# Strassen's sums of weights by their use: T2 ahead of T3, T3 fetched from memory, and the finished token half's norm behind the last operands

## The chip, the cores and the metric

The kernel runs on one core of a Trainium2 chip. The time is the device time of one launch in microseconds; a comparison takes the median of several runs of each kernel on the same chip. The engines are PE (matmuls; its weight loads are listed as PEld), DVE (vector), ACT (scalar), POOL (GpSimd) and SP. DMAs are issued from the queues of SP, ACT and POOL. Each engine works through its own list of instructions in order and waits on semaphores.

## The reference, cut to what matters

A trunk of two layers, 512 tokens of width 1024, in float32. Each layer is a mixer and a SwiGLU FFN, each with a norm before and after and a gate from a conditioning vector. The change touches the last FFN alone, from its second product on:

```python
def swiglu_ffn(h, w_in, w_out):
    gate, up = jnp.split(h @ w_in, 2, axis=-1)
    return (jax.nn.silu(gate) * up) @ w_out
...
        y = swiglu_ffn(h, f_w_in[i], f_w_out[i])
        x = x + gate * rmsnorm(y, norm_g[i, 3])
```

Here `silu(gate) * up` is 512 x 2816 and `w_out` (`w2` in the kernel) is 2816 x 1024.

## The kernel before

All matmuls are float32 products made of three matmuls on operands split in a high and a low part: ACT casts the high part, DVE subtracts it from the value to get the low part, and PE multiplies high by high, low by high and high by low.

The last product is done by a Strassen scheme with seven products in place of eight. The 22 blocks of 128 rows of `w2` make 11 pairs p = 0 to 10. Of a pair, b11 and b12 are the left and right 512 columns of its first 128 rows, b21 and b22 those of the second 128 rows. The tokens are halved likewise, 0 to 255 and 256 to 511; the activations a11 to a22 lie in `raw`, and sums of them are made by DVE in place. The table `PRODUCTS` names the seven products by the PSUM bank they add to and their two operands:

```python
    PRODUCTS = (("A", "b11", "a11"), ("B", "b21", "a12"), ("C", "b22", "a12"), ("A", "b22", "a11"),
                ("D", "b12", "s1"), ("A", "b11", "a21"), ("A", "b21", "a22"))
```

Four of the operands on the weights' side are sums, made in place, on top of blocks that were used already:

- T1: b12 becomes b12 + b11 (`t1`), used by product 4;
- T2: b22 becomes b22 + T1 (`t2_`), used by product 3;
- T3: b11 becomes the original b12 + b22 (`t3`), used by product 5;
- T4: b21 becomes b21 + T2 (`t4`), used by product 6.

Each sum is an accumulating DMA from GpSimd's queue (`add_`, L1657), with nothing computed by an engine. The weights lie in units: units 0 and 1 hold two pairs each, units 2 to 8 one each. Unit 0 to 2 are in tiles `w2t`, 3 and 4 in `w2s`, 5 to 8 in `w2h`, so the tile's name tells the unit in the profile. The sum of a unit of two pairs is one DMA of 512 KB, of one pair 256 KB; a sweep over the nine units is 2.9 MB.

There are 77 steps, each a product for one pair: 6 matmuls of 512 columns, 3 for each of two token tiles. Products with an odd number take pair 4 first (`odd`), the others go from 0 to 10. Two steps make a round n, 39 rounds. Product 3 begins with the second step of round 16, product 5 in round 27, product 6 in round 33. Product 6 adds up in bank A, which product 5 has just left. In a round n PE runs `products([n])` (L1650), then comes `behind(n)`, then `w_prep(n + 4)` splits the weights of round n + 4 (ACT L1615, DVE L1616) and `a_prep(n + 3)` the activations of round n + 3 (ACT L1628, DVE L1629). There are four buffers of split weights, so the weights of round n + 4 are split when PE is done with round n; of split activations three. The last three rounds run together, first token tile 0 of the half, then tile 1.

`behind(n)` holds what is put between the rounds: the issue of the sums, the copies and sums of finished banks (`got`), and, for the first token half, which is done after product 4 in round 27, the norm and the store. `square` gives a tile's sum of squares on ACT (L1722), `mean` and `root` make the factor (L1725, L1728, L1729), `gated` multiplies by the gate (L1732), `x_new` multiplies by the factor, adds to x and stores (L1738, L1739). In round 32 DVE takes product 5 out of bank A (L1779). The order on PE, SP, ACT, DVE and POOL in this phase is the order in which the code is written.

The T3 of before has two parts, both issued in round 2: a plain load of the original b12 over b11, on SP's queue (L1665), and the sum with b22 in the tile. T2 overwrites b22, and so comes behind T3.

Of the kernel before, what the change touches and what calls it, by code (L numbers as in the profile page):

```python
# [17 lines left out]
T = 512  # L18
# [17 lines left out]
def trunk_kernel(  # L36
# [7 lines left out]
    dma = nc.sync.dma_start  # L44
    dma_s = nc.scalar.dma_start
# [1004 lines left out]
    with ExitStack() as ph:  # L1050
# [99 lines left out]
        class Group:  # L1150
# [169 lines left out]
            def root(self):  # L1320
                self.rg = t2("rg")
                act.activation(self.rg, self.ssg, AF.Sqrt, bias=eps_t, scale=1.0 / 256)
# [219 lines left out]
    with ExitStack() as ph:  # L1542
# [14 lines left out]
        def w2_rows(p, n=1):  # L1557
            return w2[2 * p * P:(2 * p + 2 * n) * P, :].rearrange("(i c p) f -> p i c f", p=P, c=2)
# [9 lines left out]
        def b_(i, name, q=None):  # L1568

            t = rows_of[i][int(name[1]) - 1][:, :, slice(0, T) if name[2] == "1" else slice(T, D)]  # L1570
            return t if q is None else t[:, q, :]
# [81 lines left out]
        with tc.manual_schedule(engines={PE_ENGINE, mybir.EngineType.SP, mybir.EngineType.Activation,  # L1653
                                         mybir.EngineType.DVE, mybir.EngineType.Pool}):

            def add_(dst, src):
                pool.dma_start(dst, src, accum_op=ADD)  # L1657

            def t1(i):
                add_(b_(i, "b12"), b_(i, "b11"))  # L1660

            def t3(i):
                u = units[i]
                for q, p in enumerate(u):
                    dma(b_(i, "b11", q), w2_rows(p)[:, 0, 0, T:])  # L1665
                add_(b_(i, "b11"), b_(i, "b22"))

            def t2_(i):
                add_(b_(i, "b22"), b_(i, "b12"))

            def t4(i):
                add_(b_(i, "b21"), b_(i, "b22"))

            load_pair(0)
            for i, f in ((0, 0), (2, 0), (1, 1), (3, 1), (4, 2), (5, 3)):
                rest(i)
                (up if i in (2, 3) else gate)(f, lead_ps[i])
            tiles = []
            K = 2 * NF - 6
            for k in range(K):  # L1680
                if k % 2 == 0 and k < K - 4:
                    load_pair(k // 2 + 1)
                if k in (8, 14, 20):
                    w2_load((8, 14, 20).index(k))
                if k in (K - 4, K - 2):
                    w2_load(3 + (k - K + 4) // 2)
                if k in (K - 12, K - 10, K - 8):
                    t1((k - K + 12) // 2)
                tiles.append(in_chunk(ws[k], h))
                q, j = divmod(k - 3, 4)  # L1690
                if j < 2 and k > 2:
                    gate(4 + 2 * q + j, tiles[k - 1])
                elif k:
                    up(2 + 2 * q + j, tiles[k - 1])
                if k < K - 2:
                    for op in splits[k + 2]:
                        op()
                else:
                    a_prep(k - K + 2)
                    w_prep(k - K + 2)  # L1700
            up(NF - 1, tiles[-1])

            ht = [hp.tile([P, 1, D], F32, tag=f"h{j}", name=f"w2h{j}") for j in range(KD)]
            for i in range(5, len(units)):
                rows_of[i] = (ht[2 * (i - 5)], ht[2 * (i - 5) + 1])
            for c, r in ((0, 0), (0, 1), (1, 0), (1, 1)):
                for i in range(5, len(units)):
                    dma(rows_of[i][r][:, 0, c * T:(c + 1) * T], w2_rows(units[i][0])[:, 0, r, c * T:(c + 1) * T])
            for n in (2, 3):
                w_prep(n)  # L1710
            a_prep(2)
            for i in range(3, len(units)):
                t1(i)

            st = [{"s2": small(2), "s1": small(1), "b1": small(1)} for _ in range(4)]
            spare = {n: rows_of[i][0][:, 0, T:] for n, i in
                     (("junk", 3), ("gg0", 5), ("gg1", 6), ("c22_0", 7), ("c22_1", 8))}
            gg = (spare["gg0"], spare["gg1"])
            got = {}

            def square(t, part, src):
                act.activation(spare["junk"], src, AF.Square, accum_out=st[t]["s2"][:, part:part + 1])  # L1722

            def mean(t):
                dve.tensor_scalar(st[t]["b1"], st[t]["s2"][:, 0:1], 1.0 / D, EPS, MUL, ADD)  # L1725

            def root(t):
                act.activation(st[t]["s1"], st[t]["s2"][:, 1:2], AF.Sqrt, bias=st[t]["b1"], scale=1.0 / D)  # L1728
                dve.reciprocal(st[t]["s1"], st[t]["s1"])  # L1729

            def gated(src, hf, dst):
                dve.tensor_mul(dst, src, gg[hf])  # L1732
                return dst

            def x_new(t, hf, yg, parts=(FULL,), puts=(dma,)):
                for c, put in zip(parts, puts):
                    cx = slice(hf * T + c.start, hf * T + c.stop)
                    dve.scalar_tensor_tensor(xt[t][:, cx], yg[:, c], st[t]["s1"], xt[t][:, cx], MUL, ADD)  # L1738
                    put(out[0, t * P:(t + 1) * P, cx], xt[t][:, cx])  # L1739

            def behind(n):

                if n == 2:
                    for i in range(len(units)):
                        t3(i)
                for i, u in enumerate(units):
                    if n - 8 == u[-1] // 2:
                        t2_(i)
                if n == 18:
                    for i in range(len(units)):  # L1750
                        t4(i)
                for t in range(2):
                    if n == 5:
                        got["11", t] = t2("c11")
                        act.copy(got["11", t], bank["A"][t])
                    elif n == 10:
                        dve.tensor_add(got["11", t], got["11", t], bank["B"][t])
                    elif n == 16:
                        got["12", t] = t2("c12")
                        act.copy(got["12", t], bank["C"][t])  # L1760
                    elif n == 21:
                        dve.tensor_tensor(got["12", t], got["12", t], bank["A"][t], SUB)
                    elif n == 27:
                        dve.tensor_add(got["12", t], got["12", t], bank["D"][t])
                        got["22", t] = spare[f"c22_{t}"]
                        act.copy(got["22", t], bank["D"][t])
                    elif n == 28:
                        square(t, 0, got["11", t])
                        square(t, 1, got["12", t])
                        mean(t)  # L1770
                    elif n == 29:
                        root(t)
                        for hf, c in enumerate(("11", "12")):
                            gated(got[c, t], hf, got[c, t])
                    elif n == 30:
                        for hf, c in enumerate(("11", "12")):
                            x_new(t, hf, got[c, t])
                    elif n == 32:
                        dve.tensor_tensor(got["22", t], got["22", t], bank["A"][t], SUB)  # L1779
                    elif n == 33:  # L1780
                        square(2 + t, 0, got["22", t])
                        mean(2 + t)
                    elif n == 34:
                        gated(got["22", t], 1, got["22", t])

            for n in range(NT - 3):
                products([n])
                behind(n)
                if n == 26:
                    for hf in range(2):  # L1790
                        dma(gg[hf], gate_d[3, 4 * hf:4 * hf + 4].rearrange("j p -> (j p)").partition_broadcast(P))
                if n + 4 < NT:
                    w_prep(n + 4)
                if n + 3 < NT:
                    a_prep(n + 3)
            products(range(NT - 3, NT))
            for t in range(2):
                square(2 + t, 1, bank["A"][t])
                yg = gated(bank["A"][t], 0, t2("yg"))
                root(2 + t)  # L1800
                if t == 0:
                    x_new(2, 0, yg)
                    x_new(2, 1, got["22", 0])
                else:
                    x_new(3, 1, got["22", 1])
                    x_new(3, 0, yg, HALVES, (dma_s, dma))
# [29 lines left out]
```

## Time and profile before

| | us |
|---|---|
| median of 3 runs | 1376.9 (1376.27 to 1377.57) |
| the profiled execution's own time | 1379.01 |
| its span, first to last instruction | 1377.2 |
| PE busy in the span | 1345.5 |
| DVE, ACT, POOL busy | 898.0, 570.4, 46.1 |
| last FFN's second product, first matmul to the last one's end | 1238.8 to 1371.0 |

A row of the timeline gives the start and the length in us, the engine, the line of the code, the operation, the tile written and those read, the shape and the count of instructions; in brackets stands the idle time before it, and what ended it. In the lines of waits stand the sum, the count and the longest. The clock is the share of full speed granted to PE. A plain load of 256 KB by L1708 landed 3.4 to 6.2 us after its issue, one of the 11 loads by L1665 after 5.9 to 10.9 us.

### The profile page before, as it was taken

What the parts mean: (1) busy time and instruction counts of PE and PEld (TensorE: products, weight loads), DVE (VectorE), ACT (ScalarE), POOL (GpSimd) and SP (SyncE); (2) the same over time, 40 slices, a digit from 0 to 9 for tenths busy, and PEclk for the clock granted to TensorE, in tenths of its full rate; (3) what the DMA queues carried; (4) which work ended last, traced back from release to release, by engine and by line L of the source; (5) the groups of instructions that cost most, each with busy time, mean ns of one, the idle gap of its engine ahead of it and who ended that gap; (6) DMA issues with size and microseconds to landing.
All of it is one profiled execution on the core that took longest, in us unless ns stands there. A gap on an engine that the chain in (4) does not pass through costs nothing.

```text
span 1377.2 us, 17423 instructions
## 1 busy us (share of the span) xinstructions
PE 1345.5 (98%) x6909; PEld 1130.4 (82%) x6909; DVE 898.0 (65%) x1437; ACT 570.4 (41%) x893; POOL 46.1 (3%) x59
## 2 busy tenths in 40 slices
PE   8999999999999999999999999999999999999596
PEld 7788889888888888898888888888898888888485
DVE  5578766777876323768988888896743233339366
ACT  5333355232222212745555554564742212126363
POOL 0000000000000000000000000000000000002310
PEclk9999999999999999999999999999999999999798
DMA  9767751777775323333434443223402554249841
GB/s 311 227 189 240 236 178 31 244 227 240 233 248 183 123 92 91 97 100 119 138 108 138 119 126 114 85 91 108 153 31 92 168 168 130 92 131 254 142 85 61
DMA packets 160533, 204.77 MB, mean 149 GB/s; under 512 B 6836, under 2 KB 112196, under 8 KB 159428
## 3 DMA queue, kind: packets, MB, share of 16 engines
q1 hardware_dynamic: 150096, 179.23, 40.8%
q0 software_dynamic: 6208, 11.54, 4.9%
q10 hardware_dynamic: 4148, 12.90, 3.0%
q8 instruction: 54, 0.88, 0.3%
q14 instruction: 27, 0.22, 0.1%
HBM read 189.87 MB, written 2.24 MB: 139 GB/s over the span
## 4 chain that ended last, share of the span: by engine, by line
PE 91%; issue 3%; SPq 2%; DMA 1%; DVE 1%; ACT 1%; POOL 1%; DVEq 0%; POOLq 0%; ACTq 0%
PE ip L276 18%; PE ip L278 18%; PE ip L277 18%; PE y L378 6%; PE y L380 6%; PE y L379 6%; PE li L276 3%; PE li L278 3%; PE li L277 3%; PE cA L1650 2%; PE li L756 1%; PE yd L1283 1%; PE cD L1650 1%; SPq L611 1%; PE yo L1277 1%
## 5 line engine op out<-in xcount | busy, mean ns | idle before, releaser
L276 PE MATMUL ip<-h,whl 128*128 128x512 f32 x1096 | 430.8, 393 | 0.2 <-DVE cv L863 0.2
L278 PE MATMUL ip<-h,whl 128*128 128x512 f32 x1096 | 426.8, 389 | 0.0
L277 PE MATMUL ip<-h,whl 128*128 128x512 f32 x1096 | 426.5, 389 | 0.0
L222 DVE TENSOR_TENSOR whl<-wst,whl 128x1024 fp32r<-128x1024 f32 x132 | 160.7, 1221 | 133.5 <-ACT whl L221 133.4
L276 PEld LDWEIGHTS ip<-h,whl 128*128 128x128 f32 x1096 | 205.8, 188 | 43.7 <-issue 1.8
L278 PEld LDWEIGHTS ip<-h,whl 128*128 128x128 f32 x1096 | 205.7, 188 | 43.5
L277 PEld LDWEIGHTS ip<-h,whl 128*128 128x128 f32 x1096 | 205.9, 188 | 41.8
L221 ACT CAST whl<-wst 128x1024 fp32r<-128x1024 f32 x132 | 136.6, 1042 | 32.1 <-PE ip L278 23.7
L124 DVE SCALAR_TENSOR_TENSOR ada_acc<-ada_st,csil,ada_acc 128x512 f32<-128x512 f32 x140 | 105.0, 750 | 3.8 <-DMA ada_st<-in_ada_w_dram 0.3
L204 DVE TENSOR_TENSOR whlo<-wsto,whlo 128x1024 fp32r<-128x1024 f32 x41 | 49.9, 1224 | 78.4 <-ACT whlo L203 78.2
L276 PE MATMUL li<-h,whl 128*128 128x256 f32 x288 | 83.2, 289 | 0.0
L278 PE MATMUL li<-h,whl 128*128 128x256 f32 x288 | 81.6, 283 | 0.0
L277 PE MATMUL li<-h,whl 128*128 128x256 f32 x288 | 81.5, 283 | 0.0
L203 ACT CAST whlo<-wsto 128x1024 fp32r<-128x1024 f32 x41 | 42.6, 1049 | 76.3 <-PE y L380 74.8
L1650 PE MATMUL cA<-whlo,ao 128*128 128x512 f32 x264 | 64.9, 405 | 5.4 <-DVE w2h L1779 3.4
L378 PE MATMUL y<-whlo,ff 128*128 128x512 f32 x176 | 68.6, 390 | 0.0
L380 PE MATMUL y<-whlo,ff 128*128 128x512 f32 x176 | 68.5, 389 | 0.0
L379 PE MATMUL y<-whlo,ff 128*128 128x512 f32 x176 | 68.5, 389 | 0.0
L1650 PEld LDWEIGHTS cA<-whlo,ao 128*128 128x128 f32 x264 | 51.3, 196 | 18.1 <-issue 4.1
L1142 DVE SCALAR_TENSOR_TENSOR cu<-ip,cols,cu 128x511 f32<-128x511 f32 (+2 forms) x84 | 62.8, 748 | 3.9 <-ACT cu L1139 1.4
L1585 ACT ACTIVATE g<-ip 128x512 f32<-128x512 f32 x18 | 10.8, 598 | 121.9 <-PE ip L278 121.9
L276 PEld LDWEIGHTS li<-h,whl 128*128 128x128 f32 x288 | 55.3, 192 | 0.0
(278 smaller groups left out, 1931.0 us busy)
## 6 DMA issues: line engine op xcount, KB each, us to landing
ada_st<-in_ada_w_dram SPq DMA_DIRECT2D x96, 512.0 KB, 5.3
wst<-in_f_w_in_dram SPq DMA_DIRECT2D x44, 1024.0 KB, 6.4
wst<-in_m_w_in_dram SPq DMA_DIRECT2D x14, 1024.0 KB, 5.3
wsto<-in_f_w_out_dram SPq DMA_DIRECT2D x10, 1024.0 KB, 5.2
wst<-in_m_w_in_dram SPq DMA_DIRECT2D x20, 512.0 KB, 4.9
wst<-in_a_w_in_dram SPq DMA_DIRECT2D x9, 1024.0 KB, 6.1
csb<-cs_d ACTq DMA_DIRECT2D x8, 1024.0 KB, 5.1
wsto<-in_m_w_out_dram SPq DMA_DIRECT2D x7, 1024.0 KB, 6.4
```

Of the source, the lines that this page charges most:

```text
L124: dve.scalar_tensor_tensor(acc, w, csil[:, k:k + 1], acc, MUL, ADD)
L204: dve.tensor_tensor(dst[:, 1, :nk, :], src, dst[:, 0, :nk, :].bitcast(F32), SUB)
L221: later.append((lambda sw=sw, w=w: act.copy(w[:, 0, :nk, :], sw), lambda sw=sw, w=w: dve.tensor_tensor(w[:, 1, :nk, :], sw, w[:, 0, :nk, : ...
L222: lambda sw=sw, w=w: dve.tensor_tensor(w[:, 1, :nk, :], sw, w[:, 0, :nk, :].bitcast(F32), SUB)))
L276: pe.matmul(dst, w_at(w, 0, kk), a[:, 0, sl], start=start, stop=False)
L277: pe.matmul(dst, w_at(w, 0, kk), a[:, 1, sl], start=False, stop=False)
L278: pe.matmul(dst, w_at(w, 1, kk), a[:, 0, sl], start=False, stop=stop)
L378: pe.matmul(pst, a[:, 0, tk], wt[:, 0, kk, :], start=k == 0, stop=False)
L379: pe.matmul(pst, a[:, 0, tk], wt[:, 1, kk, :], start=False, stop=False)
L380: pe.matmul(pst, a[:, 1, tk], wt[:, 0, kk, :], start=False, stop=k == K - 1)
L1142: dve.scalar_tensor_tensor(u[:, sft:], pst[:, :T - sft], w[3 - sft], u[:, sft:], MUL, ADD)
L1650: pe.matmul(bank[r][sub], a[:, al, q, tk], w[:, hl, q, :], start=first and k == 0, stop=last and k == 2, skip_group_check=True)
```

## The change

T2 is issued before T3: `t2_(i)` as before in rounds 8 to 13, but with no T3 ahead of it. T3 no longer reads b22 in the tile: b11 is loaded with the original b12 by ACT's queue (`t3_load`, unit i in round 8 + i), and the sum is with the original b22 fetched from memory, pair by pair, issued in round 17. The norm of tokens 0 to 255 is spread: the squares of tile 0 in round 29, of tile 1 in round 30, `mean`, `root`, `gated` and `x_new` in rounds 34 and 35. And in the rounds from 34 on `behind` comes after `w_prep` and `a_prep`, not ahead of them. The gating of product 6's half, `gated(got["22", t], ...)`, moves from round 34 to round 35.

```diff
             def t1(i):
                 add_(b_(i, "b12"), b_(i, "b11"))
 
+            def t3_load(i):
+                for q, p in enumerate(units[i]):
+                    dma_s(b_(i, "b11", q), w2_rows(p)[:, 0, 0, T:])
+
             def t3(i):
-                u = units[i]
-                for q, p in enumerate(u):
-                    dma(b_(i, "b11", q), w2_rows(p)[:, 0, 0, T:])
-                add_(b_(i, "b11"), b_(i, "b22"))
+                for q, p in enumerate(units[i]):
+                    add_(b_(i, "b11", q), w2_rows(p)[:, 0, 1, T:])
...
             def behind(n):
 
-                if n == 2:
-                    for i in range(len(units)):
-                        t3(i)
                 for i, u in enumerate(units):
                     if n - 8 == u[-1] // 2:
                         t2_(i)
+                    if n == 8 + i:
+                        t3_load(i)
+                    if n == 17:
+                        t3(i)
                 if n == 18:
                     for i in range(len(units)):
                         t4(i)
...
-                    elif n == 28:
-                        square(t, 0, got["11", t])
-                        square(t, 1, got["12", t])
-                        mean(t)
-                    elif n == 29:
-                        root(t)
-                        for hf, c in enumerate(("11", "12")):
-                            gated(got[c, t], hf, got[c, t])
-                    elif n == 30:
-                        for hf, c in enumerate(("11", "12")):
-                            x_new(t, hf, got[c, t])
+                    elif n in (29, 30):
+                        if t == n - 29:
+                            square(t, 0, got["11", t])
+                            square(t, 1, got["12", t])
                     elif n == 32:
                         dve.tensor_tensor(got["22", t], got["22", t], bank["A"][t], SUB)
-                    elif n == 33:
+                    elif n == 34:
                         square(2 + t, 0, got["22", t])
+                        mean(t)
                         mean(2 + t)
-                    elif n == 34:
+                    elif n == 35:
+                        root(t)
                         gated(got["22", t], 1, got["22", t])
+                if n == 35:
+                    for t in range(2):
+                        for hf, c in enumerate(("11", "12")):
+                            x_new(t, hf, gated(got[c, t], hf, got[c, t]))
 
             for n in range(NT - 3):
                 products([n])
-                behind(n)
+                if n < 34:
+                    behind(n)
...
                 if n + 3 < NT:
                     a_prep(n + 3)
+                if n >= 34:
+                    behind(n)
```

GpSimd's queue behind the last T1, before. The tiles of units 0 to 2 read the same for T3 and T2, so the first three rows are T3 of units 0 to 2; of the `w2h` tiles the even ones hold b11 and b12, the odd ones b21 and b22, so a row into `w2h0` from `w2h1` is T3, and one into `w2h1` from `w2h0` is T2:

```order
L1657 DMA w2h6_9875<-w2h6_9875 128x512
L1657 DMA w2t0_8556<-w2t0_8556 128x2x512
L1657 DMA w2t1_8557<-w2t1_8557 128x2x512
L1657 DMA w2t2_8558<-w2t2_8558 128x512
L1657 DMA w2s_9736<-w2s_9736 128x512
L1657 DMA w2s_9797<-w2s_9797 128x512
L1657 DMA w2h0_9869<-w2h1_9870 128x512
```

And now, behind the same last T1, from the fourth unit on:

```order
L1657 DMA w2s_9797<-w2s_9797 128x512
L1657 DMA w2h1_9870<-w2h0_9869 128x512
L1657 DMA w2h3_9872<-w2h2_9871 128x512
L1657 DMA w2h5_9874<-w2h4_9873 128x512
L1657 DMA w2h7_9876<-w2h6_9875 128x512
L1657 DMA w2t0_8556<-in_f_w_out_dram 128x512 x2
L1657 DMA w2t1_8557<-in_f_w_out_dram 128x512 x2
L1657 DMA w2t2_8558<-in_f_w_out_dram 128x512
```

The nine sums of T2 stand where T3's nine stood, and T3's eleven follow with memory as their source; T4 follows them as it followed T2.

ACT's list in rounds 7 to 10, the difference (L1615 splits weights, L1628 activations):

```order
 L1615 CAST whlo<-w2t_8556 128x1024
 L1628 CAST ao<-raw 128x512
+L1664 DMA w2t_8556<-in_f_w_out_dram 128x512 x2
 L1615 CAST whlo<-w2t_8557 128x1024
 L1628 CAST ao<-raw 128x512
+L1664 DMA w2t_8557<-in_f_w_out_dram 128x512 x2
 L1615 CAST whlo<-w2t_8558 128x512
 L1615 CAST whlo<-w2s 128x512
 L1628 CAST ao<-raw 128x512
+L1664 DMA w2t_8558<-in_f_w_out_dram 128x512
```

The loads of T3, eleven in all, now stand between ACT's casts, one unit a round.

DVE's list at its end, before, from the last split of weights (`x_102` and `x_103` are the token tiles 2 and 3, `cA` bank A):

```order
L1616 TENSOR_TENSOR whlo<-w2h_9876,whlo 128x512
L1629 TENSOR_TENSOR ao<-raw,ao 128x512
L1629 TENSOR_TENSOR ao<-raw,ao 128x256
L1732 TENSOR_TENSOR yg<-cA_9925,w2h_9869 128x512
L1729 RECIPROCAL ss<-ss 128x1
L1738 SCALAR_TENSOR_TENSOR x_102<-yg,ss,x_102 128x512
```

And now, from the last split of activations on (`x_100` and `x_101` are the token tiles 0 and 1):

```order
L1629 TENSOR_TENSOR ao<-raw,ao 128x256
L1731 RECIPROCAL ss<-ss 128x1
L1734 TENSOR_TENSOR w2h_9873<-w2h_9873,w2h_9871 128x512
L1731 RECIPROCAL ss<-ss 128x1
L1734 TENSOR_TENSOR w2h_9875<-w2h_9875,w2h_9871 128x512
L1734 TENSOR_TENSOR c_10045<-c_10045,w2h_9869 128x512
L1740 SCALAR_TENSOR_TENSOR x_100<-c_10045,ss,x_100 128x512
L1734 TENSOR_TENSOR c_10290<-c_10290,w2h_9871 128x512
L1740 SCALAR_TENSOR_TENSOR x_100<-c_10290,ss,x_100 128x512
L1734 TENSOR_TENSOR c_10047<-c_10047,w2h_9869 128x512
L1740 SCALAR_TENSOR_TENSOR x_101<-c_10047,ss,x_101 128x512
```

Two reciprocals, six gatings and four `x_new` stand ahead of the first gating of the last two token tiles, where nothing stood before.

## The prediction

> **What bounds the kernel now.** I read the page first, then who waited for whom on PE and ACT, then the timelines of PE, POOL, ACT and DVE over the last FFN's second product, then the granted clock by windows. From the page:
>
> ```profile
> span 1377.2 us, 17423 instructions
> PE 1345.5 (98%) x6909; PEld 1130.4 (82%) x6909; DVE 898.0 (65%) x1437; ACT 570.4 (41%) x893; POOL 46.1 (3%) x59
> PEclk9999999999999999999999999999999999999798
> ```
>
> PE works in 98% of the span; only in slices 38 and 39 of 40 does its clock fall, so whatever this change can give lies there. PE's waits from 1238 us on are three, and ACT's longest stands behind the first:
>
> ```profile
> PE cC L1650 <- ACT ao L1628: 14.8, 1, 14.8
> PE cA L1650 <- DVE w2h L1779: 3.4, 1, 3.4
> PE cA L1650 <- DVE ao L1629: 2.0, 1, 2.0
> ACT whlo L1615 <- DMA w2t<-w2t: 18.4, 1, 18.4
> ```
>
> On PE's timeline the first row is the restart after the long wait; 63 matmuls then take 14.28 us (1316.42 to 1330.70), 0.2267 us each; the last row ends at 1371.0:
>
> ```profile
> 1294.59 6.33 PE L1650 MATMUL cC<-whlo,ao 128*128 128x512 f32 x15 [14.82 <-ACT ao L1628]
> ...
> 1316.42 14.44 PE L1650 MATMUL cD<-whlo,ao 128*128 128x512 f32 x63
> 1330.70 0.84 PE L1650 MATMUL cA<-whlo,ao 128*128 128x512 f32 x3
> ...
> 1353.52 17.48 PE L1650 MATMUL cA<-whlo,ao 128*128 128x512 f32 x66 [3.41 <-DVE w2h L1779]
> ```
>
> PE stopped at 1294.59 - 14.82 = 1279.77, with rounds 0 to 14 done. Steps 30 to 76 remain: 47 x 6 = 282 matmuls, 63.9 us, so an unhindered PE would end at 1343.7. It ends 27.3 us later: 20.25 us of waits, and about 7 us of slow clock, which the windows show (busy us of PE, PEld, DVE, ACT, POOL; then clock, DMA share, GB/s):
>
> ```profile
> 10.00:13.40 3.40, 2.01 (x27) 1.60 (x28) 2.13 (x7) 1.95 (x7) 0.00 (x0) 1.00 1.15 307
> ...
> 1283.50:1300.00 16.50, 5.41 (x13) 4.13 (x14) 4.93 (x7) 4.16 (x7) 7.39 (x8) 0.50 0.86 145
> ...
> 1346.60:1348.00 1.40, 1.36 (x6) 1.12 (x7) 1.40 (x3) 0.27 (x1) 0.00 (x0) 1.00 0.00 0
> 1348.10:1358.20 10.10, 6.69 (x16) 4.76 (x16) 7.80 (x14) 3.10 (x7) 0.00 (x0) 0.50 0.28 104
> ```
>
> After each wait PE runs at half clock for 5 to 7 busy us. One such stretch costs some 2.8 us: the 15 matmuls from 1294.59 to the next row at 1300.76 need 3.4 us at full clock.
>
> **T2 ahead of T3 on GpSimd's queue.** The sums today (first row T3 of unit 0, next T3 of 1 and 2; 1281.61 is T2 of unit 0, next T2 of 1 and 2; the last is T4 of unit 0):
>
> ```profile
> 1258.22 1.22 POOL L1657 DMA_DIRECT2D w2t<-w2t  x1 [3.27 <-DVE whlo L1616]
> 1266.38 2.16 POOL L1657 DMA_DIRECT2D w2t<-w2t  x2 [6.94 <-DVE whlo L1616]
> ...
> 1281.61 1.22 POOL L1657 DMA_DIRECT2D w2t<-w2t  x1 [2.27 <-issue]
> 1286.99 2.17 POOL L1657 DMA_DIRECT2D w2t<-w2t  x2 [4.16 <-issue]
> ...
> 1302.05 1.22 POOL L1657 DMA_DIRECT2D w2t<-w2t  x1 [2.28 <-issue]
> ```
>
> A sweep of 2.9 MB takes 20.4 us (1281.61 to 1302.05), 1.86 us for each 256 KB. T2 stands a whole sweep behind T3, and ACT at round 12 waits for T2 of unit 2:
>
> ```profile
> 1274.37 0.62 ACT L1615 CAST whlo<-w2h 128x512 fp32r<-128x512 f32 x1 [1.06 <-PE cC L1650]
> 1293.40 0.62 ACT L1615 CAST whlo<-w2t 128x512 fp32r<-128x512 f32 x1 [18.41 <-DMA w2t<-w2t]
> ...
> 1261.88 1.22 DVE L1616 TENSOR_TENSOR whlo<-w2t,whlo 128x1024 fp32r<-128x1024 f32 x1
> ...
> 1255.50:1261.50 6.00, 6.00 (x29) 4.95 (x28) 5.89 (x11) 3.89 (x7) 1.22 (x1) 1.00 1.08 325
> ```
>
> In the new order T2 of unit 0 waits only for the last reader of b22 there, DVE's split for product C, which ends at 1261.88 + 1.22 = 1263.1. From T2 of unit 0 to ACT's release there are 11.8 us now (1281.61 to 1293.40). Alone, it would land at 1275.0. The upper end: beside SP's loads (the window above moves 325 GB/s, the DMA engines full) T3 of unit 0 held up the next for 8.2 us (1258.22 to 1266.38) against 5.4 for T2's (1281.61 to 1286.99); 11.8 x 8.2 / 5.4 = 17.9, landing at 1281.0. PE comes to round 15 at 1279.77 and started 1.2 us after the cast (1293.40 to 1294.59), so the cast must start by 1278.6. The lateness is -3.6 to +2.4 us. ACT now issues the T3 loads, 512 KB in rounds 8 and 9 and then 256 KB a round of 2.72 us, 94 GB/s, under a third of that window's rate: nearer to the lower end. I enter 0.5 us. Later units have more room: T2 of unit 8 follows a sweep later, by about 1283 (1263.1 + 20.4), and lands near 1288, when round 17 asks for it, two rounds before PE does.
>
> **T3 and T4 behind it.** T3 then runs from about 1285 to 1305, T4 to 1326 with its last landing at 1331. Round r ends at 1274.3 + 2.72 (r - 12). T3's last unit is cast in round 28 (1317.8), T4's in round 34 (1334.1), and PE needs each about 4 us later: 12 and 7 us to spare, if a sum with its source in memory goes at the pace of one within the chip. No row shows such a sum. The bounds are 1.86 us, the pace above, and the landing time, if they go one by one:
>
> ```profile
> w2h<-w2h POOLq DMA_DIRECT2D x16, 256.0 KB, 5.0
> ```
>
> I take 1.86: the sums move the same pieces, and plain loads from memory ran faster than the sums (325 GB/s). Up to 2.5 us the slack covers it.
>
> **Loads on ACT's queue.** 11 issues at about 0.35 us (the ACTq row below). ACT idles 1.06 us in a round (bracket of the 1274.37 row), two issues take 0.7: hidden, and if not, ACT is late by tenths against two rounds of split weights. Taking them from SP gains nothing: no one waits for SP there. POOL gets two more sums to issue and is 3% busy.
>
> **The norm of tokens 0 to 255.** Squares, root and gating leave rounds 28 to 30:
>
> ```profile
> 1340.60 1.28 ACT L1728 ACT_TABLE_LOAD   x1
> 1341.90 0.48 ACT L1728 ACTIVATE ss<-ss 128x1 f32<-128x1 f32 x2
> ...
> 1342.31 1.27 DVE L1732 TENSOR_TENSOR c<-c,w2h 128x512 f32<-128x512 f32 x2
> ...
> 1346.50 2.73 DVE L1738 SCALAR_TENSOR_TENSOR x<-c,ss,x 128x512 f32<-128x512 f32 x4
> ...
> 1316.38 1.27 DVE L1762 TENSOR_TENSOR c<-c,cA 128x512 f32<-128x512 f32 x2
> ```
>
> That takes the 2.0 us wait, and most of the 3.4. What is late next is round 33, where product T4 reuses bank A while DVE must first read it (L1779). In round 21, with no norm about, the same read began at 1316.38, when PE was free at 1316.42: its first half ends 0.64 later, so a PE that needed the bank would wait 0.8 us with a semaphore's 0.15. The far end is today's 3.4. The squares stay in rounds 29 and 30, two in each, 1.5 us by their rows (1336.05 and 1336.80 start the first two) against 1.06 of idle:
>
> ```profile
> 1336.05 0.63 ACT L1722 ACTIVATE w2s<-c 128x512 f32<-128x512 f32 x1
> ...
> 1336.80 0.63 ACT L1722 ACTIVATE w2s<-c 128x512 f32<-128x512 f32 x1
> ```
>
> So DVE, which follows ACT, is up to 0.8 us later by round 31: I take 1.6 us, nearer to round 21's row.
>
> **The tail.** What left the rounds now stands on DVE ahead of the last two tiles:
>
> ```profile
> 1364.23 0.41 ACT L1628 CAST ao<-raw 128x256 fp32r<-128x256 f32 x1 [1.58 <-PE cA L1650]
> ...
> 1368.42 0.69 DVE L1732 TENSOR_TENSOR yg<-cA,w2h 128x512 f32<-128x512 f32 x1 [3.31 <-ACT w2s L1722]
> ...
> 1369.88 0.74 DVE L1738 SCALAR_TENSOR_TENSOR x<-w2h,ss,x 128x512 f32<-128x512 f32 x1
> 1371.76 0.69 DVE L1732 TENSOR_TENSOR yg<-cA,w2h 128x512 f32<-128x512 f32 x1 [1.13 <-ACT w2s L1722]
> ...
> 1373.22 0.87 DVE L1738 SCALAR_TENSOR_TENSOR x<-yg,ss,x 128x256 f32<-128x256 f32 x2
> ...
> 1373.73 0.35 ACTq L1739 DMA_DIRECT2D out_dram<-x  x1
> ```
>
> The last cast starts 6.8 us before PE's end (1364.23, 1371.0). From it: 0.4 + 1.3 table + 0.3 root = 2.0; two reciprocals and two gatings 1.5; four gatings and four x_new 2 x 1.27 + 2.73 = 5.3; tile 2 2.2 (1368.42 to 1370.6); tile 3 2.3 (1371.76 to 1374.1). That is 13.3, some 0.2 less for overlapping ends: DVE ends 6.3 us after PE, where it was 3.1. Bounds: 5.5 and 7. Behind DVE the last store takes the same 3.1 us (1374.1 to 1377.2).
>
> **The sum.** 1343.7 + 0.5 + 1.6 + 6.3 + 3.1 = 1355.2, 22.0 us under this span. The profiled execution took 1379.0 us in all, 2.1 over the runs' median of 1376.9; its own time would be 1357.0, the median 1354.9.
>
> **Rivals.** (1) T2 is late by the full 2.4 us: the price is 2.4 - 0.5 + 2.8 for the clock, 1359.6. For it: T3's 8.2 us beside loads; against: a third of the load. (2) The 1.6 us at round 33 halve the clock: +2.8, 1357.7. For it: after the 2.0 us wait at 1344.6 the clock was still 1.00 in 1346.60:1348.00 and 0.50 from 1348.1; against: in 10.00:13.40 PE worked 2.01 of 3.40 us and kept 1.00. The Trainium skill, "TensorE: Matmul & The Clock Gate", section "HAM oscillation — how this bites in real kernels", warns of PE gaps over about 3.4 us only. By that rule this rival falls and the time stays 1354.9; the trace disagrees, a 2.0 us wait was enough, so the rival keeps its chance. (3) Sums from memory take 3.7 us: T3 ends at 1326, T4's last lands at 1351, 13 us after PE needs it; with one slow stretch +16, 1371. (4) The other side: they go one by one, 5.0 us each. T3 ends at 1340, T4's last lands at 1365.5, 27.5 us late; with two slow stretches +33, 1388, slower. It decides from about 4 us a sum on (11 x (4.0 - 1.86) - 7 = 17 us late, and 5.6 for the clock). Against both: no row hints that memory is the slower source. (5) T2 starts no earlier than now, because POOL is held by something other than T3: the long wait stays and only the norm's waits go (2.0 + 1.8 + 3.4 of clock, less 3.2 of tail), 1372.9. Against: the order leaves only DVE and sums eight places earlier before it.
>
> **Chances.** Forecast 0.58; (1) 0.17; (2) 0.12; (3) 0.06; (4) 0.04; (5) 0.03. The range runs from 1352 (no wait at rounds 15 and 33, tail 5.5) to 1361.5 (rivals 1 and 2 in part together), leaving 3, 4, 5 and some edges out. A difference of 0.2%, 2.8 us, is what a measurement can tell from none: faster 0.94, same 0.02, slower 0.04.
>
> **What would show it.** Right: no PE wait of over 3 us after 1238; T2 of unit 0 at about 1263 on POOL, T3 from about 1285; clock 1.00 to the end; PE ending near 1346, DVE 6 us behind. Wrong: ACT waiting for a sum anywhere; POOL's T3 rows more than 2.5 us apart; a clock of 0.50 before the end; DVE's list ending later than 7 us after PE.

## The result, and the profile after

The changed kernel takes 1357.14 us (median of four runs, 1356.92 to 1357.37) where the kernel before, beside it, took 1377.24 (1376.27 to 1377.61): a ratio of 0.9855, with a 95% interval of 0.9838 to 0.9872. It is faster by 20.1 us. The profiled execution took 1357.08 us, with a span of 1355.3.

The page of the changed kernel, its span, its engines and the granted clock in 40 slices:

```profile
span 1355.3 us, 17419 instructions
PE 1339.1 (99%) x6909; PEld 1126.9 (83%) x6909; DVE 898.7 (66%) x1437; ACT 570.1 (42%) x893; POOL 47.0 (3%) x61
PEclk9999999999999999999999999999999999999998
```

The clock no longer falls in slice 38, and PE is busy 6.4 us less for the same 6909 matmuls: what went there is work at half clock. PE's waits from 1235 us on, and ACT's for sums of weights (in all, count, longest):

```profile
PE cA L1650 <- ACT whlo L1615: 0.8, 1, 0.8
PE cC L1650 <- ACT ao L1628: 0.3, 1, 0.3
```

```profile
ACT whlo L1615 <- DMA w2t<-w2t: 3.9, 1, 3.9
ACT whlo L1615 <- DMA w2h<-w2h: 2.7, 4, 1.7
```

Of 20.2 us of waits on PE 1.1 are left. ACT still waits 3.9 us for a sum; PE feels 0.3 of it. PE's timeline around the two places:

```profile
1279.95 4.05 PE L1650 MATMUL cC<-whlo,ao 128*128 128x512 f32 x15 [0.33 <-ACT ao L1628]
1283.84 0.84 PE L1650 MATMUL cA<-whlo,ao 128*128 128x512 f32 x3
...
1330.33 15.22 PE L1650 MATMUL cA<-whlo,ao 128*128 128x512 f32 x66 [0.77 <-ACT whlo L1615]
```

PE stopped at 1279.62. The next 15 matmuls need 3.40 us at 0.2267 each, and the row behind them starts at 1283.84, 4.22 later: round 15 lost 0.8 us in all, with the clock full, since its operands came piece by piece: PE's weight loads wait 0.75 us for ACT's cast of the activations and then 0.51 us more for DVE's low part. PE ends at 1345.55. GpSimd's queue, the first three T2 rows, the ends of T3 from memory and of T4:

```profile
1263.40 1.22 POOL L1657 DMA_DIRECT2D w2t<-w2t  x1 [10.84 <-DVE whlo L1616]
1272.34 2.16 POOL L1657 DMA_DIRECT2D w2t<-w2t  x2 [7.71 <-DVE ao L1629]
...
1288.88 0.89 POOL L1657 DMA_DIRECT2D w2t<-in_f_w_out_dram  x1 [1.58 <-issue]
...
1308.66 0.86 POOL L1657 DMA_DIRECT2D w2h<-in_f_w_out_dram  x1 [3.33 <-issue]
1312.10 1.22 POOL L1657 DMA_DIRECT2D w2t<-w2t  x1 [2.58 <-issue]
...
1329.36 0.86 POOL L1657 DMA_DIRECT2D w2h<-w2h  x1 [0.46 <-issue]
```

T2 of unit 0 starts when DVE's split is done, and holds up the next for 8.9 us (1263.40 to 1272.34). The eleven sums from memory take ten steps in 19.78 us, 1.98 us each. And ACT's cast of T2 of unit 2, which waited for it, and of the last T4, which did not; then DVE's end, the reading of bank A first:

```profile
1278.76 0.62 ACT L1615 CAST whlo<-w2t 128x512 fp32r<-128x512 f32 x1 [3.91 <-DMA w2t<-w2t]
...
1336.07 0.62 ACT L1615 CAST whlo<-w2h 128x512 fp32r<-128x512 f32 x1 [1.06 <-PE cA L1650]
```

```profile
1329.50 1.28 DVE L1775 TENSOR_TENSOR w2h<-w2h,cA 128x512 f32<-128x512 f32 x2
...
1347.72 0.68 DVE L1734 TENSOR_TENSOR yg<-cA,w2h 128x512 f32<-128x512 f32 x1
1351.30 0.88 DVE L1740 SCALAR_TENSOR_TENSOR x<-yg,ss,x 128x256 f32<-128x256 f32 x2
```

DVE ends at 1352.18, 6.6 us behind PE, and the last store 3.1 us later.

### The profile page after: what moved, and what is told of

It reads as the page before. It is cut to its first block, busy times and chain, and to the rows that moved or that the text cites. A ratio compares the mean times of both kernels' runs of the same rounds, so it can differ in the third digit from the quotient of the medians.

```text
span 1355.3 us, 17419 instructions
## 1 busy us (share of the span) xinstructions
PE 1339.1 (99%) x6909; PEld 1126.9 (83%) x6909; DVE 898.7 (66%) x1437; ACT 570.1 (42%) x893; POOL 47.0 (3%) x61
## 4 chain that ended last, share of the span: by engine, by line
PE 93%; issue 2%; SPq 2%; DMA 1%; DVE 1%; ACT 1%; POOL 0%; DVEq 0%; POOLq 0%; ACTq 0%
PE ip L276 19%; PE ip L278 18%; PE ip L277 18%; PE y L378 6%; PE y L379 6%; PE y L380 6%; PE cA L1650 3%; PE li L276 3%; PE li L278 3%; PE li L277 3%; PE li L756 1%; PE yd L1283 1%; PE cD L1650 1%; SPq L611 1%; PE yo L1277 1%
## 5 line engine op out<-in xcount | busy, mean ns | idle before, releaser
L1650 PE MATMUL cA<-whlo,ao 128*128 128x512 f32 x264 | 61.1, 390 | 0.8 <-ACT whlo L1615 0.8
```

The lines of the kernel that those rows point to most:

```text
L1650: pe.matmul(bank[r][sub], a[:, al, q, tk], w[:, hl, q, :], start=first and k == 0, stop=last and k == 2, skip_group_check=True)
```

## The experiments

A ratio is against the kernel before, run beside each on the same chip (medians there 1377.77 for the first four, 1377.25 for the others).

**The sums alone.** The changed kernel with the norm where it stood before (the cut shows its first part; `x_new`, the last half's norm and the place of `behind` are put back likewise):

```diff
-                    elif n in (29, 30):
-                        if t == n - 29:
-                            square(t, 0, got["11", t])
-                            square(t, 1, got["12", t])
+                    elif n == 28:
+                        square(t, 0, got["11", t])
+                        square(t, 1, got["12", t])
+                        mean(t)
+                    elif n == 29:
+                        root(t)
+                        for hf, c in enumerate(("11", "12")):
+                            gated(got[c, t], hf, got[c, t])
...
```

> The changed kernel with the old norm: tokens 0 to 255 are squared in round 28, rooted in 29, stored in 30, and behind(n) comes ahead of the splits again. Theory (the sums' order took the long wait and its slow clock; the norm was a separate, small matter): no PE wait at round 15 beyond 0.5 us, but the old waits at rounds 31 to 33 come back, 2.0 and 3.4 us, with a stretch at half clock that costs about 3.4, while the tail shrinks from 6.6 to 3.1 us behind PE's end. PE ends at 1345.6 + 5.4 + 3.4 - 0.8 = 1353.6, the span is 1359.8, the time 1361.6. Rival (the norm's waits were a late echo of the long wait, since everything behind it ran late, and go with it): no wait over 1 us at rounds 31 to 33, PE ends at 1345, the span is 1351, the time 1353, better than the change.

It took 1361.6 us (1361.01 to 1362.01), ratio 0.9882 (0.9868 to 0.9897), with a span of 1359.2. PE's waits:

```profile
PE cA L1650 <- DVE w2h L1782: 2.8, 1, 2.8
PE cA L1650 <- DVE ao L1629: 2.0, 1, 2.0
```

The long wait is gone, and the two that stand behind the norm are there, as in the kernel before: the theory holds, and the norm's waits were no echo of the long one. Most of the gain, some 16 us, is the sums'. Against the changed kernel's span 3.9 us more: waits 4.8 for 1.1, two windows at half clock with 6.6 us of PE's work in them (half of which, 3.3, is lost), less 3.5 of the tail (DVE ends 3.1 us behind PE here, 6.6 there), which makes 3.7 + 3.3 - 3.5 = 3.5; 0.4 us of the difference stay without an account.

**The norm alone.** The kernel before with the norm spread as in the changed one:

```diff
-                    elif n == 28:
+                    elif n in (29, 30):
+                        if t == n - 29:
...
-                    elif n == 34:
+                    elif n == 35:
+                        root(t)
                         gated(got["22", t], 1, got["22", t])
+                if n == 35:
+                    for t in range(2):
+                        for hf, c in enumerate(("11", "12")):
+                            x_new(t, hf, gated(got[c, t], hf, got[c, t]))
```

> The kernel before with the new place of the norm alone; T3 stands ahead of T2 as it did. Theory: the 14.8 us wait at round 15 stays with its slow clock (2.8 us), the waits of 2.0 and 3.4 us become one of 0.8, their slow clock goes, the tail grows by 3.5 us: the span falls from 1377.2 by 5.4 - 0.8 + 3.4 - 3.5 = 4.5 to 1372.7, the time is about 1373 to 1374. Rival (what the tail takes is all that the rounds gain): within 1 us of the kernel before.

It took 1372.52 us (1372.25 to 1373.61), ratio 0.9961 (0.9947 to 0.9975). PE's waits:

```profile
PE cC L1650 <- ACT ao L1628: 14.6, 1, 14.6
PE cA L1650 <- ACT whlo L1615: 0.8, 1, 0.8
```

The span is 1371.8, where 1372.7 were expected, and the rival, no gain, falls. So the norm's move takes the 2.0 us away and 0.8 remains of the other, with or without the sums' new order. The parts give 16.2 and 5.3 us by their medians, some 21.4 together, and the whole 20.1: they add up within the intervals, which are about 2 us to either side for each.

**T3 from memory, but ahead of T2.** The changed kernel with T3's loads on SP and its sums issued in round 2:

```diff
-                    dma_s(b_(i, "b11", q), w2_rows(p)[:, 0, 0, T:])
+                    dma(b_(i, "b11", q), w2_rows(p)[:, 0, 0, T:])
...
+                if n == 2:
+                    for i in range(len(units)):
+                        t3_load(i)
+                        t3(i)
                 for i, u in enumerate(units):
                     if n - 8 == u[-1] // 2:
                         t2_(i)
-                    if n == 8 + i:
-                        t3_load(i)
-                    if n == 17:
-                        t3(i)
```

> The changed kernel with T3 fetched from memory as now, but with its loads on SP's queue and its sums on GpSimd's issued in round 2, ahead of T2, as before. Theory (it is the order on GpSimd's queue): T2 of unit 0 is issued at 1279 to 1283 in place of 1263.4, PE waits 13 to 16 us at round 15 and loses 2.8 to the clock, the span is 1355.3 + 13 to 18 = 1368 to 1373, the time 1370 to 1375. Rival (it is the source: T2 had waited for T3 to read b22 in the tile, and a T3 from memory leaves T2 free wherever it stands): T2 goes beside it, no wait over 3 us, the time stays near 1357 to 1360.

It took 1371.6 us (1371.42 to 1373.14), ratio 0.9958 (0.9943 to 0.9973). PE's wait, and on POOL the first T3 and the first T2:

```profile
PE cC L1650 <- ACT ao L1628: 12.9, 1, 12.9
```

```profile
1255.90 0.88 POOL L1657 DMA_DIRECT2D w2t<-in_f_w_out_dram  x1 [1.48 <-DVE ao L1629]
...
1279.23 1.22 POOL L1657 DMA_DIRECT2D w2t<-w2t  x1 [2.80 <-issue]
```

T2 comes as late as forecast, the wait is a little under the 13 to 16 us expected, and the rival, the source, falls. What the sums gain is the order on the queue. The source in memory gives little by itself: 1371.6 us beside 1372.52 for the norm alone, and a wait of 12.9 for 14.6. Its part is to let T2 overwrite b22 before T3.

**T3's loads earlier.** Two mechanisms could have held up T2 of units 1 and 2 by 8.9 us: the loads on ACT's queue beside it, or DVE, named as POOL's releaser. In the changed kernel only the rounds of the loads are moved:

```diff
-                    if n == 8 + i:
+                    if n == (3, 4, 5, 5, 6, 6, 7, 7, 7)[i]:
                         t3_load(i)
```

> The changed kernel with the eleven loads of T3 issued by ACT in rounds 3 to 7, while GpSimd's queue is nearly empty, in place of rounds 8 to 16. Theory (T2 of unit 0 held up the next for 8.9 us, 1263.40 to 1272.34, since the loads share the DMA engines with it): that interval falls to 5.4 to 6 us, T2 of unit 2 lands by 1275.5, the 0.33 us wait at round 15 and the half microsecond of late low parts behind it go; the span falls by 0.8 us to 1354.5, the time to 1356.3. All later sums come 3 us earlier and ACT's waits for sums go. Rival (DVE, busy without a break until 1269, holds back GpSimd's descriptors): the interval stays 8 to 9 us, the wait stays, the time stays at 1357.1.

It took 1355.9 us (1355.6 to 1356.22), ratio 0.9841 (0.9827 to 0.9856). T2 on POOL, ACT's wait, and PE's only wait:

```profile
1263.48 1.22 POOL L1657 DMA_DIRECT2D w2t<-w2t  x1 [10.27 <-DVE whlo L1616]
1269.37 2.16 POOL L1657 DMA_DIRECT2D w2t<-w2t  x2 [4.67 <-DVE c L1760]
```

```profile
ACT whlo L1615 <- DMA w2t<-w2t: 0.9, 1, 0.9
```

```profile
PE cA L1650 <- ACT whlo L1615: 0.8, 1, 0.8
```

The second T2 now starts 5.9 us after the first, not 8.9, with DVE busy for 5.2 of these 5.9 us: the loads slowed the sum, DVE did not hold the queue. ACT waits 0.9 us for a sum, PE waits for none, and PE ends 0.85 us earlier (1344.70). The gain is read from the two profiles; the intervals of the two ratios overlap.

**The tail taken apart.** On top of that kernel, the gating and the roots of tokens 0 to 255 go to rounds 33 and 34, and only `x_new` and the gating of product 6's half stay in round 35:

```diff
-                        mean(t)
...
+                if n in (33, 34):
+                    t = n - 33
+                    if n == 33:
+                        mean(0)
+                        mean(1)
+                    for hf, c in enumerate(("11", "12")):
+                        gated(got[c, t], hf, got[c, t])
+                    if n == 33:
+                        root(0)
+                        root(1)
                 if n == 35:
                     for t in range(2):
                         for hf, c in enumerate(("11", "12")):
-                            x_new(t, hf, gated(got[c, t], hf, got[c, t]))
+                            x_new(t, hf, got[c, t])
+                    for t in range(2):
+                        gated(got["22", t], 1, got["22", t])
...
-                if n < 34:
+                if n < 33:
...
-                if n >= 34:
+                if n >= 33:
```

> The kernel with the early loads, and the first half's norm spread over the rounds: mean, root and the gating of tile 0 in round 33, the gating of tile 1 in round 34, the four x_new and the gating of product 6's half in round 35, all behind the rounds' splits. Theory (the tail, 6.6 us behind PE's end where it was 3.1, is DVE's twelve operations behind the last operands): DVE has 4.2 us of it left in the 6.8 us until PE's end, the tail goes back to 3.1 us, PE's end stays at about 1344.7; the span falls by 3.5 us from 1354.4 to 1350.9, the time from 1355.9 to 1352.4. Rival (four gatings of 0.6 us in rounds 33 and 34 are more than DVE has to spare there, about 0.8 us a round, and PE waits for split operands): a wait of 1 us or more in rounds 35 to 38, a gain under 2 us.

It took 1353.08 us (1352.7 to 1353.53), ratio 0.9825 (0.9812 to 0.9838): 2.8 us under the kernel it starts from, where 3.5 were expected. The two were measured on different chips, on which the kernel before differs by 0.5 us; the spans of the two profiles differ by 3.3 (1354.4 and 1351.1). PE ends at 1344.33, and its only wait is 0.8 us as before, so the rival falls. DVE's timeline at the end:

```profile
1339.64 2.74 DVE L1740 SCALAR_TENSOR_TENSOR x<-c,ss,x 128x512 f32<-128x512 f32 x4
1342.29 1.29 DVE L1734 TENSOR_TENSOR w2h<-w2h,w2h 128x512 f32<-128x512 f32 x2
...
1345.62 0.68 DVE L1734 TENSOR_TENSOR yg<-cA,w2h 128x512 f32<-128x512 f32 x1
...
1347.07 0.88 DVE L1740 SCALAR_TENSOR_TENSOR x<-yg,ss,x 128x256 f32<-128x256 f32 x2
```

The tail falls from 6.6 to 3.6 us (1347.95 less 1344.33). It does not reach 3.1, because DVE still works without a break up to the last tile's gating; the next of its work would have to leave round 35 too.

**Bank A read earlier.** The trace names a cast of ACT (L1615) as what ended the 0.77 us in round 33, the prediction named DVE's reading of bank A. On top of the last kernel, `a_prep(34)` goes ahead of the weights' splits in round 32, out of round 31's list:

```diff
+                if n == 32:
+                    a_prep(34)
                 if n + 4 < NT:
                     w_prep(n + 4)
-                if n + 3 < NT:
+                if n + 3 < NT and n != 31:
                     a_prep(n + 3)
```

> The same, and in round 31 the split of activations for round 34 is put off behind DVE's reading of bank A in round 32. Theory (PE's 0.8 us wait at round 33 is DVE's backlog of one split, 0.6 us, ahead of that reading, although the trace names an ACT cast): the wait falls from 0.78 to about 0.2 us, the span by 0.6 us against the kernel with the norm spread. Rival (it is the cast that the trace names, L1615, split weights that come late): the wait stays at 0.7 to 0.8 us and the time is the same.

It took 1352.54 us (1352.03 to 1353.81), ratio 0.9822 (0.9808 to 0.9835), the lowest of all, though the runs overlap with those of the kernel it starts from. PE's only wait, then its last restart, the reading of bank A and ACT's cast:

```profile
PE cA L1650 <- DVE w2h L1775: 0.2, 1, 0.2
```

```profile
1328.92 15.22 PE L1650 MATMUL cA<-whlo,ao 128*128 128x512 f32 x66 [0.17 <-DVE w2h L1775]
...
1328.09 1.38 DVE L1775 TENSOR_TENSOR w2h<-w2h,cA 128x512 f32<-128x512 f32 x2
...
1328.79 0.62 ACT L1615 CAST whlo<-w2s 128x512 fp32r<-128x512 f32 x1 [1.05 <-PE cA L1650]
```

The wait falls when DVE's list in front of the reading is shorter, and now the trace names DVE. PE stops at 1328.75 here, 0.66 us after the reading began; in the kernel with the norm spread it stopped at 1328.32, 0.05 after (1328.27). ACT's cast did not move: it starts 0.04 us after PE's stop in both (1328.79 and 1328.36), and here PE goes on before the cast ends. The wait fell by 0.6 us as forecast, but the span fell by 0.2 and not by 0.6: in this profile PE was 0.43 us later already at the start of product C (1268.75 against 1268.32), ahead of what was changed. In the changed kernel too the times fit the reading: it starts at 1329.50, its first half ends 0.64 later, and PE goes on at 1330.33.

**The kernel before, twice more.** The saving against the median came out 1.9 us under the forecast though the sum for the span was right, so the question was whether the price of a wait is a constant. Nothing is edited.

> The kernel before, unchanged, for another profile. The execution that the prediction's sum was made against took 1379.0 us, 1.3 us more than any of the runs listed beside it. Theory A (the clock's raising after a wait falls on a grid of about 3.4 us, so the same waits cost more in one execution than in another; the prediction took one execution's price): the waits are 14 to 15, 2.0 and 2.8 to 3.4 us as before, but the stretches at half clock differ by 1 us or more, and so does the span, between 1374.5 and 1377.5. Theory B (T2's landing varies): the wait at round 15 differs by 1 us or more. Theory C (all executions under the profile carry the 2 us, and the changed kernel's too): span 1377.2 and time 1379.0 again.

> The same once more, a third execution of the kernel before, with the same three theories: A, other lengths of half clock with the same waits; B, another wait at round 15; C, again 1377.2 and 1379.0.

They took 1379.31 and 1376.4 us. PE's restarts after the three waits, in the first and then in the second:

```profile
1294.59 6.52 PE L1650 MATMUL cC<-whlo,ao 128*128 128x512 f32 x15 [14.45 <-ACT ao L1628]
...
1346.83 2.55 PE L1650 MATMUL cA<-whlo,ao 128*128 128x512 f32 x10 [2.01 <-DVE ao L1629]
...
1353.71 17.58 PE L1650 MATMUL cA<-whlo,ao 128*128 128x512 f32 x66 [4.34 <-DVE w2h L1779]
```

```profile
1293.95 5.10 PE L1650 MATMUL cC<-whlo,ao 128*128 128x512 f32 x15 [14.30 <-ACT ao L1628]
...
1344.75 4.13 PE L1650 MATMUL cA<-whlo,ao 128*128 128x512 f32 x10 [2.01 <-DVE ao L1629]
...
1351.63 16.80 PE L1650 MATMUL cA<-whlo,ao 128*128 128x512 f32 x66 [2.75 <-DVE w2h L1779]
```

The same 2.01 us wait, and the ten matmuls behind it take 2.55 us in the one and 4.13 in the other. The granted clock says why. In windows of 3.413 us, laid on the instants at which it changes (busy us of PE, PEld, DVE, ACT, POOL, then clock, DMA share, GB/s), the first window of each holds all or most of the 2.0 us wait; first the profile of before that the prediction used, then the first new one, then the second:

```profile
1344.66:1348.07 3.41, 1.44 (x6) 1.20 (x7) 3.41 (x6) 2.21 (x5) 0.00 (x0) 1.00 0.00 0
1348.07:1351.49 3.42, 2.04 (x6) 1.03 (x4) 3.42 (x6) 1.35 (x3) 0.00 (x0) 0.50 0.81 307
1351.49:1354.90 3.41, 1.38 (x3) 1.17 (x4) 3.41 (x7) 1.76 (x5) 0.00 (x0) 0.50 0.00 0
```

```profile
1345.08:1348.49 3.41, 1.66 (x7) 1.41 (x8) 3.41 (x5) 1.98 (x4) 0.00 (x0) 1.00 0.05 20
1348.49:1351.90 3.41, 0.89 (x4) 0.39 (x3) 3.41 (x6) 1.66 (x3) 0.00 (x0) 1.00 0.77 287
```

```profile
1341.31:1344.72 3.41, 1.43 (x6) 0.68 (x5) 3.41 (x7) 3.41 (x7) 0.00 (x0) 1.00 0.00 0
1344.72:1348.14 3.42, 3.39 (x8) 2.72 (x9) 3.42 (x5) 0.25 (x1) 0.00 (x0) 0.50 0.57 213
1348.14:1351.55 3.41, 0.73 (x3) 0.26 (x2) 3.41 (x7) 1.69 (x4) 0.00 (x0) 1.00 0.25 94
```

Where PE was busy for 1.43 or 1.44 us of a window, the next ran at half clock; where it was busy for 1.66, the next stayed full. In the second new profile PE works a whole window at half clock, and the one after it is full again; in the profile of before the half-clock window itself held only 2.04 us of work, and the next stayed at half. So the clock's changes do fall on a grid, as theory A has it, and a 2.0 us wait does not always halve the clock. What A said of the waits missed: the last is 4.34 us in the first new profile, where 2.8 to 3.4 were expected. B falls, since the waits at round 15 (14.82, 14.45, 14.30) differ by half a microsecond, and C falls with the 1376.4 us.

The half clock on those ten matmuls cost nothing, though. From the restart after the 2.0 us wait to the last restart there are 6.89, 6.88 and 6.88 us in the three profiles (1346.63 to 1353.52, 1346.83 to 1353.71, 1344.75 to 1351.63): whatever PE loses there it waits less for DVE, whose reading of bank A begins 6.05 to 6.06 us after the first of the two restarts in all three. The executions part elsewhere, behind the long wait. These are the windows in which PE restarts there, in the same order, all of them at half clock:

```profile
1293.46:1296.87 3.41, 2.28 (x5) 1.70 (x6) 2.64 (x4) 3.41 (x6) 2.40 (x3) 0.50 0.97 163
```

```profile
1293.88:1297.29 3.41, 2.70 (x6) 2.04 (x7) 3.07 (x5) 3.41 (x7) 1.98 (x3) 0.50 1.07 180
```

```profile
1293.52:1296.94 3.42, 2.99 (x7) 2.29 (x8) 3.25 (x6) 3.40 (x6) 1.75 (x3) 0.50 1.07 180
```

Behind the first two, with 2.28 and 2.70 us of work, the next window stayed at half clock; behind the third, with 2.99, it was full. So the 15 matmuls take 6.17, 6.36 and 4.94 us up to the next row (1300.76, 1300.95 and 1298.89), and in the same way the last 66 take 17.48, 17.58 and 16.80.

The times follow these two stretches. PE ends at 1371.0 in the profile that the prediction used, at 1371.29 and 1368.43 in the two new ones: 27.3, 27.6 and 24.7 us behind an unhindered PE. Of these, waits are 20.2, 20.8 and 19.1 (14.3, 2.0 and 2.8 in the last), and the rest, 7.1, 6.8 and 5.6, is mostly clock. The executions took 1379.0, 1379.3 and 1376.4 us, 8.0 us behind PE's end each time. Of the 2.9 us between the two new ones the two stretches make 2.2 (1.42 and 0.78), an earlier stop before the long wait 0.5.

That the other executions of the kernel before differ for the same reason is not shown; only their mean granted clock is on record. It fits: of the 17 beside the experiments, the seven at 0.992, as in the 1376.4 us profile, took 1376.34 to 1377.91 us, six of them 1377.04 or less, and the ten at 0.989 or 0.991 took 1377.25 to 1378.84. But it is not the only thing that moves the time: the last kernel above, at 0.999 in all four runs, spreads from 1352.03 to 1353.81.

## Why the prediction was right, and where it was off

- The order on the queue: right. T2 of unit 0 starts at 1263.4 (1263.1 forecast), and its third unit is cast at 1278.76, within 1275.0 to 1281.0. That cast was 0.2 us behind the 1278.6 worked out; round 15 lost 0.8 us where 0.5 was entered. Rival 1's mechanism, the loads beside the sums, is real: T2's step is 8.9 us with the loads and 5.9 without, from T2 of unit 0 to the cast there were 15.4 us, between the bounds of 11.8 and 17.9, and not nearer the lower one, as the prediction had put it. It had judged by 256 KB of loads a round, but rounds 8 and 9 carry 512 KB each, and just these stand beside T2 of unit 0: all DMAs together moved 196 GB/s from 1263.40 to 1266.10, and 92 in the 5.9 us of the kernel with the loads early. The price of the lateness at round 15 was a third of the rival's 2.4 us.
- T3 from memory: right. 1.98 us a sum, beside the 1.86 taken and far from the 3.7 and 5.0 of rivals 3 and 4. T3 began at 1288.9, not at 1285, since T2 was slowed; T4's last row, at 1329.4, was still early enough, for ACT's cast of round 34 waited for PE alone. Issuing the loads on ACT's queue moved nothing that PE felt; what they did to T2 stands above.
- Rival 5 fell at the first row: POOL was free.
- Round 33: the direction right, the size too dear. 1.6 us were entered for the squares' knock-on, 0.77 measured, which is the lower row (0.8): ACT, without a break from 1316.46 on, had caught up with the squares by 1326.87, where it waits for PE again. Rival 2, the half clock behind it, did not come up. The Trainium skill ("TensorE: Matmul & The Clock Gate", "HAM oscillation — how this bites in real kernels") warns of gaps of over some 3.4 us; of the 2.0 us waits here three halved the clock (the prediction's profile, the second new one of before, and the sums alone) and one did not. The share of the window decided, so the rule's number would have been too lax for the clock of the kernel before.
- The tail: 6.6 us for 6.3, and the 3.1 of the store right.
- The sum: 1355.2 for the span against 1355.3, 1357.0 for the execution's own time against 1357.08. That it comes within 0.1 us is in part luck: three errors, 0.8 too much at round 33 and 0.3 too little each at the tail and at round 15, nearly cancel.
- The step that failed is the last of the sum. "2.1 over the runs' median" was taken off the changed kernel's time too, as if the profiled execution were slower by something that the change leaves. Measured, the changed kernel's profiled execution lay at its median (1357.08 and 1357.14), all four runs within 0.25 us. So the saving is 22 us against that one execution and 20.1 against the median. The 2.8 us for a slow stretch was one execution's price too: behind the long wait it is 2.8, 3.0 and 1.5 us in the three profiles. Of the three traced executions of before, the two dear ones were dear by half-clock windows behind waits that the change removes or shortens; that the distance from the median of the others comes from there is likely, and not shown.

## What to carry to other kernels

When sums or loads share one in-order queue, put them in the order of their use, and where a data hazard forbids it, look for another source of the operand. Work that moves out of one engine's tight rounds should be spread over later slack, not stacked at the end: 3.5 us of what the norm's move gave were paid back in the tail, and 2.8 came back once it was spread. And when a change removes waits that may have made the profiled execution dear, forecast its time from that execution alone, and the saving from the median; do not carry the execution's distance from the median over.

## What the runs showed of the hardware

- In these traces, from 1238 us on, the granted clock changed only on a grid of 3.413 us windows whose place differs from execution to execution. After a full-clock window with PE busy 1.47 us or less of 3.41 (0.43, the sums alone) the next ran at half clock; from 1.66 (0.49) it stayed full. From half clock it rose after a window with 2.99 us of work or more, not after one with 2.70 or less. Waits so have a price that depends on their phase: 2.55 and 4.13 us for the same ten matmuls, where the next wait took the difference back, and 4.94 and 6.36 us for the same 15, where nothing did.

```profile
1325.91:1329.32 3.41, 1.47 (x7) 0.73 (x5) 3.41 (x7) 3.41 (x7) 1.32 (x2) 1.00 1.04 177
1329.32:1332.74 3.42, 3.34 (x8) 2.67 (x9) 3.42 (x6) 0.30 (x1) 0.91 (x2) 0.50 0.91 197
```

These are the windows of the sums alone, in the form of those above.

- A sum of 512 KB on GpSimd's queue with plain loads beside it held up the next for 8.9 us, without them for 5.9; a sum with its source in memory kept the pace of one within the chip, 1.98 against 1.86 us for 256 KB.
- The releaser that the trace names need not be the one: ACT's cast stood for the 0.77 us that DVE's reading of the bank ended, as the run that moved the reading ahead shows (0.17 us in place of 0.77).
